# A two-layer encoder trunk: first stage ordered by hand, with operands in PSUM, and per-block statistics in the second layer

## The chip, the cores and the metric

The kernel runs on one NeuronCore of one Trainium2 chip. The metric is the device time of one execution in microseconds, the median of several runs. Engines are named TensorE (PE in the rows), VectorE (DVE), ScalarE (ACT), GpSimd (POOL) and SyncE (SP, which issues the DMAs).

## The reference

512 tokens of width 1024 go through two layers. A conditioning vector c gives per layer six vectors of shifts, scales and gates, `silu(c) @ w_mod + b_mod`. In each layer:

```
h = rms_norm(x, g) * (1 + scale1) + shift1
[q_d | k_d | v_d | c_q | c_kv | k_rope] = h @ w_in
o_d = 8 heads of dilated windowed attention, ALiBi by position, q and k normed per head
o_m = 8 heads of latent attention: normed c_q and c_kv projected up, a rotary key shared by the heads
x = x + gate1 * (concat[o_d, o_m] @ w_out)
h = rms_norm(x, g') * (1 + scale2) + shift2
x = x + gate2 * (relu(h @ w1) ** 2 @ w2)
```

All is float32. The positions are integers; the angles of the rotary part are position times inverse frequency.

## The kernel before

x is kept transposed, eight tiles x0 to x7 of 128 channels by 512 tokens. Every product that needs float32 accuracy is made of three: each operand is split into a high part (a copy to a short format, on ScalarE, L233) and the rest (a subtraction on GpSimd, L234), and `mm3` (L237 to L240) multiplies high by high, low by high and high by low.

The conditioning takes 96 blocks of 512 KB of `w_mod`. silu(c) is spread over all partitions as a row `cb` of 1024 elements: the diagonal of each piece is multiplied by ones on TensorE into PSUM, and ScalarE copies the bank to SBUF (L112 to L118). One VectorE instruction multiplies a block by `cb` and sums it (L170).

The **first stage** (L694 to L753) norms x and projects it. It first sums the squares of x (ScalarE squares, VectorE adds, L122 to L128) while GpSimd works out the rotary angles (L135 to L147) and ScalarE their sine and cosine (L150, L151), for which it loads another set of tables and then loads the set for Ln and Exp again (L152). The inverse norm (`inv_rms`, L244 to L251) is 512 columns wide and ends in an SBUF tile y. Then a loop goes over the eight chunks of 128 channels. Per chunk: two blocks of `w_mod` are multiplied on VectorE (a scale and a shift), u = x times y on VectorE (L719), the high part of h on ScalarE (L732), all of h on ScalarE (L733), the low part on VectorE for one chunk and on GpSimd for the next (L723, L735), and 24 products on TensorE: four blocks of tokens of the first dilated head pair (384 columns, four banks `mm`) and four of the latent projection (416 columns, two banks `sc` and two banks `tr`). For every second chunk the weights are loaded and split.

After the loop come the statistics of the first dilated pair (`chain` in `dil_prep`, L428 to L451: squares, a reduction over two blocks, the small inverse root `rsqrt_tiny` of L221 to L226 with Ln and Exp, a scaling), its transposes (`tail`), the same for the latent part with the rotary key and its tables (`tail` in `latent`, L521 to L542), and the distances of positions (L305 to L325). Then eight steps, one per head pair, run the attention (`heads`, `head`); in each the projection of a later pair, weight loads and blocks of `w_mod` are placed by `weave` at positions from a table. `head` makes scores into a bank `sc` (L472, L473), adds a bias (L339, L343), takes the softmax, transposes it into a bank `tr` (L358), splits it (L361, L362) and multiplies it with the values (L368).

A scheduler orders each engine's instructions by a simulated timeline, within the data's dependences and the buffers' numbers; only VectorE's order in the chunk loop, and some single instructions, are fixed by hand to the order in the program. Tiles with a tag share as many buffers as BUFS gives the tag; a new one waits until an old one is read for the last time.

Of the kernel before, what the change touches and what calls it, by code (L numbers as in the profile page):

```python
# [16 lines left out]
L = 2  # L17
# [25 lines left out]
def trunk(ctx: ExitStack, tc: tile.TileContext, a):  # L43
# [28 lines left out]

    def ps(tag, shape=(128, 512)):
        return psum.tile(list(shape), F32, tag=tag, bufs=BUFS[tag], name=nm(tag))
# [20 lines left out]
    SY.dma_start(inv, bass.AP(tensor=a["inv"].tensor, offset=a["inv"].offset, ap=[[0, 128], [1, 16]]))  # L95
# [8 lines left out]


# [5 lines left out]
    cb = const.tile([128, D], F32, name="cb")  # L111
    for i in range(2):  # L112
        p = ps("sc", (128, 4, 128))
        dg = s2([128, 4, 128])
        for k in range(4):
            V.tensor_scalar(dg[:, k], ident, cs[:, 4 * i + k:4 * i + k + 1], None, op0=OP.mult)
        T.matmul(p.rearrange("p k c -> p (k c)"), ones, dg.rearrange("p k c -> p (k c)"), start=True, stop=True)
        A.activation(cb[:, 512 * i:512 * i + 512], p.rearrange("p k c -> p (k c)"), AF.Copy)  # L118


    sq0 = s2(tag="o")
    for j in range(8):  # L122
        if j == 0:
            A.activation(sq0, xT[j], AF.Square)
        else:
            sq = s2(tag="P")
            A.activation(sq, xT[j], AF.Square)
            V.tensor_tensor(sq0, sq0, sq, op=OP.add)  # L128


    pf = col(4, "pf")
    V.tensor_copy(pf, posc)
    ang, kf, w_ = s2([128, 4, 16]), s2([128, 4, 16]), s2([128, 4, 16], tag="b")
    for t in range(4):
        G.tensor_scalar(ang[:, t], inv, pf[:, t:t + 1], 0.0, op0=OP.mult, op1=OP.add)  # L135
    G.tensor_scalar(kf, ang, 1.0 / (2 * math.pi), 12582912.0, op0=OP.mult, op1=OP.add)
    G.tensor_scalar(kf, kf, -12582912.0, 0.0, op0=OP.add, op1=OP.add)
    c1 = 6.28125
    c2 = float(np.float32(np.round((2 * math.pi - c1) * 2.0 ** 20) / 2.0 ** 20))
    c3 = 2 * math.pi - c1 - c2  # L140
    for cc in (c1, c2, c3):
        G.tensor_scalar(w_, kf, -cc, 0.0, op0=OP.mult, op1=OP.add)
        G.tensor_tensor(ang, ang, w_, op=OP.add)
    PI_ = 3.1415925
    G.tensor_scalar(ang, ang, PI_, -PI_, op0=OP.min, op1=OP.max)
    A.activation(kf, ang, AF.Abs)
    G.tensor_scalar(kf, kf, -1.0, math.pi / 2, op0=OP.mult, op1=OP.add)  # L147
    sin = const.tile([128, 4, 16], F32, name="sin")
    cos = const.tile([128, 4, 16], F32, name="cos")
    A.activation(sin, ang, AF.Sin)  # L150
    A.activation(cos, kf, AF.Sin)  # L151
    pre = A.preload_act_table_set("natural_log_exp_and_others")  # L152
    tc.keep_in_program_order(pre)
    ctx.enter_context(tc.issue_after(pre.ins))
# [7 lines left out]
    def mod_block(l, i, tag="raw", pool_=False, pin=False, out=None):  # L162
        out = modc[l][:, i:i + 1] if out is None else out
        w = t4(tag, [128, D], F32)
        SY.dma_start(w, a["wmod"][l, i])
        if pool_:
# [25 lines left out]
    def first_norm(j):  # L192

        A.activation(modc[0][:, j:j + 1], mraw[:, j:j + 1], AF.Identity, bias=cols[0][:, C_BMOD + j:C_BMOD + j + 1])
        A.activation(amix[0][:, j:j + 1], mraw[:, 8 + j:9 + j], AF.Identity, bias=gb0[:, j:j + 1],
                     scale=cols[0][:, C_GMIX + j:C_GMIX + j + 1])

# [31 lines left out]
    def load_split(src, n, raw="raw"):  # L229
        raw = t4(raw, [128, 1024], F32)[:, :n]  # L230
        hi, lo = t4("wh", [128, 1024])[:, :n], t4("wl", [128, 1024])[:, :n]
        SY.dma_start(raw, src)
        A.activation(hi, raw, AF.Copy)  # L233
        G.tensor_tensor(lo, raw, f(hi), op=OP.subtract)  # L234
        return hi, lo
# [8 lines left out]
    def inv_rms(p, v, y, t):  # L244

        V.tensor_scalar(v, p, 1.0 / D, EPS, op0=OP.mult, op1=OP.add)
        A.activation(t, v, AF.Ln)
# [3 lines left out]
        V.scalar_tensor_tensor(y, t, 1.5, p, op0=OP.add, op1=OP.mult)  # L251
# [52 lines left out]
    def distances():  # L304

        posr = s2([128, S], I32)
        SY.dma_start(posr, bass.AP(tensor=a["pos"].tensor, offset=a["pos"].offset, ap=[[0, 128], [1, S]]))
# [10 lines left out]
        dist = [t4("ot", [128, 2, S], F32) for _ in range(2)]  # L318
        for qb in range(4):
# [3 lines left out]
        g = t4("ot", [128, 896], F32)  # L323
        SY.dma_start(g, a["lnc"])
        return dist, g  # L325
# [52 lines left out]
    for l in range(L):  # L378
# [19 lines left out]
        def group(src, n):  # L398
            ws = {}

            def load(i, raw="raw"):
                hi, lo = load_split(src[i], 2 * n, raw)
                ws[i] = (hi.rearrange("p (k n) -> p k n", k=2), lo.rearrange("p (k n) -> p k n", k=2))

# [4 lines left out]
            return [lambda i=i, **kw: load(i, **kw) for i in range(4)], step  # L409
# [13 lines left out]
        def dil_prep(pr, k_outer=False):  # L423
            w = dict(mm=[], chain=[])
            w["load"], step = group(a["win"][l, pr], 384)
            R = {}

            def chain(tb, bank):  # L428
# [4 lines left out]
                if t == 0:  # L433
                    R[half] = t4("pt" if k_outer else "zz", [128, 2, 4, 2, 64], F32)
                    R["sq"], R["bank"] = s2([128, 8, 64]), bank
                sq = R["sq"]
                A.activation(sq[:, 4 * t:4 * t + 4].rearrange("p h d -> p (h d)"), bank[:, 0:256], AF.Square, scale=1.0 / 8)
                src = bank[:, 256:384].rearrange("p (h d) -> p h d", h=2)
                vt = R["VD"][:, tb]
                A.activation(vt[:, :, 0], src, AF.Copy)  # L440
                V.tensor_tensor(vt[:, :, 1], src, f(vt[:, :, 0]), op=OP.subtract)
                if t == 0:
                    return

                v = small(8)
                V.tensor_reduce(v, sq, axis=AX.X, op=OP.add)
                rs = rsqrt_tiny(v, 8, bank)
                for u, bk in enumerate((R["bank"], bank)):
                    src = bk[:, 0:256].rearrange("p (h o d) -> p h o d", h=4, o=1).to_broadcast([128, 4, 2, 64])
                    scl = rs[:, 4 * u:4 * u + 4].rearrange("p (h o d) -> p h o d", o=1, d=1).to_broadcast([128, 4, 2, 64])  # L450
                    V.tensor_tensor(R[half][:, u], src, scl, op=OP.mult)  # L451
# [48 lines left out]
        def latent():  # L500
            w = dict(mm=[], chain=[])
            w["load"], step = group(a["winc"][l], W_C)
# [191 lines left out]
        if l == 0:  # L694
# [9 lines left out]
            def u_of(k):  # L704
                return us[k // 2][:, k % 2]
# [240 lines left out]
```

## Time and profile before

| what | us |
|---|---|
| median of 3 runs | 1368.05 |
| lowest and highest | 1367.66, 1368.26 |
| the profiled execution | 1368.62 |
| its span in the trace | 1366.8 |
| TensorE busy | 1275.1 (93%) |
| VectorE busy | 752.4 (55%) |
| ScalarE busy | 673.9 (49%) |
| GpSimd busy | 651.0 (48%) |

Times in the trace count from the start of the span. Busy time of TensorE is of pipelined products: one product's duration overlaps the next one's, so their pace is read from the distances of their starts. The first stage lies from 0 to about 80 us, the attention of the first layer to about 340, its second half to about 730, and the second layer behind it.

### The profile page before, as it was taken

What the parts mean: (1) busy time and instruction counts of PE and PEld (TensorE: products, weight loads), DVE (VectorE), ACT (ScalarE), POOL (GpSimd) and SP (SyncE); (2) the same over time, 40 slices, a digit from 0 to 9 for tenths busy, and PEclk for the clock granted to TensorE, in tenths of its full rate; (3) what the DMA queues carried; (4) which work ended last, traced back from release to release, by engine and by line L of the source; (5) the groups of instructions that cost most, each with busy time, mean ns of one, the idle gap of its engine ahead of it and who ended that gap; (6) DMA issues with size and microseconds to landing.
All of it is one profiled execution on the core that took longest, in us unless ns stands there. A gap on an engine that the chain in (4) does not pass through costs nothing.

```text
span 1366.8 us, 19167 instructions
## 1 busy us (share of the span) xinstructions
PE 1275.1 (93%) x6922; PEld 1109.2 (81%) x6922; DVE 752.4 (55%) x1588; ACT 673.9 (49%) x1389; POOL 651.0 (48%) x504
## 2 busy tenths in 40 slices
PE   3879979898899999999998999999889999999999
PEld 2878867787888888888898988788688888888888
DVE  6677888876661752825574566987662122121223
ACT  5567888875532332322344766887654133232321
POOL 5636785571554444444443533454145444444441
PEclk7989999999999999999999999999999999999999
DMA  9325552331163663845522433211013223223321
GB/s 344 111 95 170 181 164 90 118 124 63 63 224 115 218 229 103 294 142 188 170 82 63 132 124 111 74 45 62 1 63 108 93 93 108 93 93 100 101 93 62
DMA packets 57247, 167.59 MB, mean 123 GB/s; under 512 B 8641, under 2 KB 10817, under 8 KB 57153
## 3 DMA queue, kind: packets, MB, share of 16 engines
q1 hardware_dynamic: 57152, 166.38, 37.0%
q8 instruction: 54, 0.88, 0.3%
q14 instruction: 41, 0.33, 0.1%
HBM read 155.87 MB, written 10.49 MB: 122 GB/s over the span
## 4 chain that ended last, share of the span: by engine, by line
PE 72%; DVE 6%; ACT 5%; issue 4%; POOL 4%; DMA 3%; POOLq 0%; DVEq 0%; ACTq 0%
PE mm L238 21%; PE mm L239 21%; PE mm L240 21%; PE tr L368 3%; PE tr L358 2%; POOL wl L234 2%; DMA raw<-in_wout_dram 1%; DVE pt L362 1%; ACT wh L233 1%; DVE P L343 1%; POOL raw L167 1%; PE sc L238 1%; PE mm L459 1%; PE sc L239 1%; PE sc L240 1%
## 5 line engine op out<-in xcount | busy, mean ns | idle before, releaser
L234 POOL TENSOR_TENSOR wl<-raw,wh 128x1024 fp32r<-128x1024 f32 (+3 forms) x188 | 425.4, 2266 | 449.6 <-ACT wh L233 431.4
L233 ACT ACTIVATE wh<-raw 128x1024 fp32r<-128x1024 f32 (+3 forms) x188 | 189.0, 1005 | 273.7 <-PE mm L240 206.4
L649 DVE SCALAR_TENSOR_TENSOR x<-mm,mod,x 128x512 f32<-128x512 f32 (+1 forms) x144 | 89.1, 629 | 259.9 <-PE mm L240 259.5
L238 PE MATMUL mm<-h,wh 128*128 128x512 f32 (+1 forms) x608 | 224.5, 370 | 7.1 <-ACT h L274 7.1
L239 PE MATMUL mm<-h,wl 128*128 128x512 f32 (+1 forms) x608 | 224.6, 370 | 0.0
L240 PE MATMUL mm<-h,wh 128*128 128x512 f32 (+1 forms) x608 | 221.7, 369 | 1.1 <-POOL h L271 1.1
L238 PE MATMUL mm<-ot,wh 128*128 128x512 f32 (+1 forms) x448 | 154.1, 347 | 4.9 <-ACT ot L641 4.1
L239 PE MATMUL mm<-ot,wl 128*128 128x512 f32 (+1 forms) x448 | 153.1, 344 | 0.0
L240 PE MATMUL mm<-ot,wh 128*128 128x512 f32 (+1 forms) x448 | 150.7, 346 | 0.6 <-POOL ot L642 0.6
L822 ACT ACTIVATE P<-mm 128x512 f32<-128x512 f32 (+1 forms) x72 | 39.2, 551 | 203.9 <-PE mm L240 203.9
L238 PEld LDWEIGHTS mm<-h,wh 128*128 128x128 f32 x608 | 116.2, 191 | 26.1 <-ACT h L274 7.5
L239 PEld LDWEIGHTS mm<-h,wl 128*128 128x128 f32 x608 | 116.1, 191 | 19.0 <-POOL wl L234 0.3
L240 PEld LDWEIGHTS mm<-h,wh 128*128 128x128 f32 x608 | 114.5, 190 | 20.3 <-POOL h L271 1.6
L823 DVE SCALAR_TENSOR_TENSOR mm<-mm,P 128x512 f32<-128x512 f32 (+1 forms) x72 | 45.4, 636 | 138.6 <-ACT P L822 138.6
L238 PE MATMUL mm<-wh,h 128*128 128x384 f32 (+1 forms) x288 | 98.7, 357 | 15.8 <-ACT h L732 9.8
L239 PE MATMUL mm<-wh,h 128*128 128x384 f32 (+1 forms) x288 | 101.8, 354 | 5.1 <-POOL h L735 3.6
L238 PE MATMUL mm<-qk,wh 128*128 128x512 f32 (+1 forms) x288 | 105.3, 366 | 1.0 <-DVE x L649 1.0
L239 PE MATMUL mm<-qk,wl 128*128 128x512 f32 (+1 forms) x288 | 105.2, 365 | 0.0
L240 PE MATMUL mm<-qk,wh 128*128 128x512 f32 (+1 forms) x288 | 105.2, 365 | 0.0
L355 POOL TENSOR_SCALAR P<-P,hs 128x512 f32<-128x512 f32 x64 | 48.4, 756 | 116.5 <-DVE hs L348 94.8
L240 PE MATMUL mm<-wl,h 128*128 128x384 f32 (+1 forms) x288 | 100.2, 351 | 0.0
L170 DVE SCALAR_TENSOR_TENSOR pt<-pt,cb 128x1024 f32<-128x1024 f32 x56 | 99.1, 1804 | 0.0
(248 smaller groups left out, 2667.1 us busy)
## 6 DMA issues: line engine op xcount, KB each, us to landing
raw<-in_w_dram SPq DMA_DIRECT2D x64, 512.0 KB, 3.3
pt<-in_wmod_dram SPq DMA_DIRECT2D x56, 512.0 KB, 4.8
raw<-in_w2a_dram SPq DMA_DIRECT2D x48, 512.0 KB, 3.4
raw<-in_wmod_dram SPq DMA_DIRECT2D x24, 512.0 KB, 3.6
raw<-in_win_dram SPq DMA_DIRECT2D x30, 384.0 KB, 3.2
bias<-b SPq DMA_DIRECT2D x32, 256.0 KB, 2.1
raw<-in_wout_dram SPq DMA_DIRECT2D x16, 512.0 KB, 3.4
raw<-in_w2b_dram SPq DMA_DIRECT2D x16, 512.0 KB, 3.3
```

The lines of the kernel that those rows point to most:

```text
L170: r = V.scalar_tensor_tensor(w, w, 1.0, cb, op0=OP.mult, op1=OP.mult, accum_out=out)
L233: A.activation(hi, raw, AF.Copy)
L234: G.tensor_tensor(lo, raw, f(hi), op=OP.subtract)
L238: T.matmul(out, sh, mh, start=first, stop=False)
L239: T.matmul(out, sl, mh, start=False, stop=False)
L240: T.matmul(out, sh, ml, start=False, stop=last)
L355: G.tensor_scalar(P, P, r_, 0.0, op0=OP.mult, op1=OP.add)
L358: T.transpose(tr[:, kc], P[:, kc * 128:(kc + 1) * 128], ident)
L368: T.matmul(po[:, HALF[qh]], vals(hd, kc), pt[qh][w][:, kc], start=(kc == 0 and w == 0), stop=(kc == 3 and w == 1))
L649: V.scalar_tensor_tensor(xT[j][:, hf], p, gt[:, j:j + 1], xT[j][:, hf], op0=OP.mult, op1=OP.add)
L822: A.activation(r, p, AF.Relu)
L823: V.scalar_tensor_tensor(p, p, 0.0, r, op0=OP.max, op1=OP.mult)
```

## The change

In the first stage the order of SP, VectorE, ScalarE and GpSimd is now the program's, written out by hand. The row cb stays in PSUM through the chunk loop (`cbp`, in a tile `trp` of two banks that replaces the two `tr` buffers; later uses of tag `tr` take its halves by turns), and ScalarE copies it to SBUF only behind the loop. The inverse norm stays in PSUM too; its Ln reads the bank itself, with scale and bias. The sum of squares is kept in PSUM until its last addition, and two of the squares are made by GpSimd. The low part of h is made by GpSimd for every chunk. The blocks of `w_mod` come in eight buffers in place of sixteen; the splits of the latent weights use other buffers for the first half.

In the loop, TensorE makes the four blocks of the dilated pair and one block of the latent projection; its other three blocks follow behind the loop, one in the bank that the norm leaves and two in banks `mm`. The angles, the sine (one operation for sine and cosine, with both loads of tables) and the distances stand behind the loop, on VectorE and ScalarE. The tables of the rotary key and the key itself (`rope`) move into the second attention step of layer 1. In layer 2 the dilated statistics are worked out for each block of 128 tokens, where they were for two together.

The diff, cut to its core:

```diff
+    trp = psum.tile([128, 2, 512], F32, name="trp")
+    turn = [0]
     def ps(tag, shape=(128, 512)):
+        if tag == "tr":
+            turn[0] ^= 1
+            v = trp[:, turn[0]]
+            return v.rearrange("p (a b) -> p a b", a=shape[1]) if len(shape) == 3 else v
...
-    cols = [col(N_COL, f"cols{l}") for l in range(L)]
-    SY.dma_start(cols[0], a["cols"][0])
-    posc = const.tile([128, 4], I32, name="posc")
-    SY.dma_start(posc, a["pos"].rearrange("(t p) -> p t", p=128))
-    inv = col(16, "inv")
-    SY.dma_start(inv, bass.AP(tensor=a["inv"].tensor, ...))
     xT = [const.tile([128, S], F32, name=f"x{j}") for j in range(8)]
     for j in range(8):
         SY.dma_start(xT[j], a["xT"][j])
+    cols = [col(N_COL, f"cols{l}") for l in range(L)]
+    SY.dma_start(cols[0], a["cols"][0])
...
+    cbp = trp.rearrange("p a b -> p (a b)")
     for i in range(2):
...
-        A.activation(cb[:, 512 * i:512 * i + 512], p.rearrange("p k c -> p (k c)"), AF.Copy)
+        T.matmul(cbp[:, 512 * i:512 * i + 512], ones, dg.rearrange("p k c -> p (k c)"), start=True, stop=True)
...
+    def rotary():
+        pf = col(4, "pf")
+        V.tensor_copy(pf, posc)
+        ang, kf = sin, cos
+        for t in range(4):
+            V.tensor_scalar(ang[:, t], inv, pf[:, t:t + 1], None, op0=OP.mult)
+        V.tensor_scalar(kf, ang, 1.0 / (2 * math.pi), 12582912.0, op0=OP.mult, op1=OP.add)
+        V.tensor_scalar(kf, kf, -12582912.0, None, op0=OP.add)
...
+        for cc in (c1, c2, c3):
+            V.scalar_tensor_tensor(ang, kf, -cc, ang, op0=OP.mult, op1=OP.add)
...
+        A.activation(sines, sines, AF.Sin)
+        exp_tables()
...
-    def inv_rms(p, v, y, t):
+    def inv_rms(p, v, t):
+        A.activation(t, p, AF.Ln, bias=epsc, scale=1.0 / D)
         V.tensor_scalar(v, p, 1.0 / D, EPS, op0=OP.mult, op1=OP.add)
-        A.activation(t, v, AF.Ln)
         A.activation(p, t, AF.Exp, scale=-0.5)
...
-        V.scalar_tensor_tensor(y, t, 1.5, p, op0=OP.add, op1=OP.mult)
+        V.scalar_tensor_tensor(p, t, 1.5, p, op0=OP.add, op1=OP.mult)
...
-    def distances():
-        posr = s2([128, S], I32)
+    def distances(posr):
...
+        rotary()
         for qb in range(4):
...
+                nb = 2 if l == 0 else 1
+                if t == 0 or nb == 1:
+                    R["sq"], R["bank"] = s2([128, 4 * nb, 64]), []
...
+                if len(got) == nb:
+                    v = small(4 * nb)
+                    V.tensor_reduce(v, sq, axis=AX.X, op=OP.add)
+                    rs = rsqrt_tiny(v, 4 * nb, bank)
+                    for u, (t_, bk) in enumerate(got):
...
+                        V.tensor_tensor(R[half][:, t_], src, scl, op=OP.mult)
...
+            with tc.manual_schedule(engines={E.SP, E.DVE, E.Activation, E.Pool}):
+                for k in range(8):
+                    mods(k)
+                    if k % 2 == 0:
+                        weights(k // 2)
+                    if k == 2:
+                        SY.dma_start(posc, a["pos"].rearrange("(t p) -> p t", p=128))
...
+                sq0, sqp = s2(tag="o"), ps("mm")
+                A.activation(sqp, xT[0], AF.Square)
+                for j in range(1, 8):
+                    sq = s2(tag="P")
+                    if j in (1, 4):
+                        G.tensor_tensor(sq, xT[j], xT[j], op=OP.mult)
+                    else:
+                        A.activation(sq, xT[j], AF.Square)
+                    V.tensor_tensor(sq0 if j == 7 else sqp, sqp, sq, op=OP.add)
+                T.matmul(p, ones, sq0, start=True, stop=True)
+                banks = [ps("mm") for _ in range(4)]
+                lbanks = [ps("sc")]
+                splits(0)
+                mod_mul(8)
+                mod_mul(0)
+                inv_rms(p, v, t)
+                for k in range(8):
...
+                    V.tensor_tensor(u, xT[k], p, op=OP.mult)
+                    first_norm(k)
+                    A.activation(hi, u, AF.Identity, bias=be, scale=ga)
+                    A.activation(u, u, AF.Identity, bias=be, scale=ga)
+                    G.tensor_tensor(lo, u, f(hi), op=OP.subtract)
+                    if k % 2 == 0 and k < 6:
+                        splits(k // 2 + 1)
                     if k < 7:
...
+                        mod_mul(9 + k)
+                        mod_mul(k + 1)
+                    for tb in range(4):
+                        PR[0]["step"](banks[tb][:, :384], k, tb)
+                    W["step"](lbanks[0][:, :W_C], k, 0)
+                gains()
+                dist = distances(posr)
+                for i in range(2):
+                    A.activation(cb[:, 512 * i:512 * i + 512], cbp[:, 512 * i:512 * i + 512], AF.Copy)
+            lbanks.append(ps("sc"))
+            for k in range(8):
+                W["step"](lbanks[1][:, :W_C], k, 1)
+            g = t4("ot", [128, 896], F32)
+            SY.dma_start(g, a["lnc"])
+            bias0 = dist, g
+            for fn in PR[1]["load"][:2]:
+                fn(keep=True)
             for tb in range(4):
                 PR[0]["do_chain"](tb, banks[tb])
+            for tb in (2, 3):
+                lbanks.append(ps("mm"))
+                for k in range(8):
+                    W["step"](lbanks[tb][:, :W_C], k, tb)
...
+            if l == 0 and st == 1:
+                ev += [(2, W["rope"])]
```

## Rows read from the trace of the kernel before

**Rows 1.** stages; busy PE, PEld, DVE, ACT, POOL; clock, DMA share, GB/s

```profile
25.50:70.30 44.80, 39.94 (x192) 37.30 (x192) 33.75 (x46) 24.93 (x47) 28.87 (x23) 0.92 0.46 165
70.30:79.40 9.10, 4.13 (x19) 3.40 (x20) 7.79 (x22) 6.69 (x29) 3.30 (x2) 0.81 0.46 151
79.40:100.00 20.60, 18.55 (x88) 17.61 (x87) 15.36 (x44) 12.47 (x37) 8.00 (x9) 0.83 0.21 74
100.00:180.00 80.00, 74.88 (x464) 69.52 (x462) 64.70 (x153) 63.86 (x146) 56.55 (x41) 0.98 0.52 171
180.00:220.00 40.00, 30.31 (x197) 24.52 (x194) 30.57 (x86) 35.73 (x86) 34.19 (x35) 0.91 0.50 156
```

**Rows 2.** TensorE in order of time: start us, us, engine, line, operation

```profile
25.55 0.69 PE L238 MATMUL mm<-wh,h 128*128 128x384 f32 x1 [9.48 <-ACT h L732]
...
69.76 0.35 PE L239 MATMUL tr<-wh,h 128*128 128x416 f32 x1
69.94 0.35 PE L240 MATMUL tr<-wl,h 128*128 128x416 f32 x1
...
79.43 0.47 PE L472 MATMUL sc<-qk,qk 128*128 128x512 f32 x1
```

**Rows 3.** ScalarE in order of time, front of the program and last chunk

```profile
15.60 1.28 ACT L150 ACT_TABLE_LOAD   x1
...
19.82 0.61 ACT L247 ACTIVATE b<-b 128x512 f32<-128x512 f32 x1
...
24.68 0.81 ACT L732 ACTIVATE h<-pt,mod,am 128x512 fp32r<-128x512 f32 x1 [2.98 <-DVE pt L728]
...
59.62 0.81 ACT L732 ACTIVATE h<-pt,mod,am 128x512 fp32r<-128x512 f32 x1
```

**Rows 4.** VectorE's groups, 24 to 60 us: count, busy us, mean ns

```profile
L170 DVE SCALAR_TENSOR_TENSOR qk<-qk,cb 128x1024 f32<-128x1024 f32 x7 | 11.5, 1646 | 0.0
L170 DVE SCALAR_TENSOR_TENSOR ot<-ot,cb 128x1024 f32<-128x1024 f32 x7 | 9.6, 1374 | 0.0
L719 DVE TENSOR_TENSOR pt<-x,P 128x512 f32<-128x512 f32 x7 | 9.1, 1304 | 0.0
L723 DVE TENSOR_TENSOR h<-pt,h 128x512 fp32r<-128x512 f32 x4 | 4.1, 1037 | 1.4 <-ACT pt L733 1.4
```

**Rows 5.** VectorE in order of time, chunk loop

```profile
24.56 0.68 DVE L719 TENSOR_TENSOR pt<-x,P 128x512 f32<-128x512 f32 x1
...
45.03 0.68 DVE L719 TENSOR_TENSOR pt<-x,P 128x512 f32<-128x512 f32 x1
45.64 1.21 DVE L170 SCALAR_TENSOR_TENSOR qk<-qk,cb 128x1024 f32<-128x1024 f32 x1
```

**Rows 6.** GpSimd in order of time, end of the chunk loop

```profile
58.14 2.82 POOL L234 TENSOR_TENSOR wl<-zz,wh 128x768 fp32r<-128x768 f32 x1
...
63.98 1.85 POOL L234 TENSOR_TENSOR wl<-raw,wh 128x768 fp32r<-128x768 f32 x1
...
65.79 1.28 POOL L735 TENSOR_TENSOR h<-pt,h 128x512 fp32r<-128x512 f32 x1
```

**Rows 7.** VectorE's largest group from 100 to 300 us

```profile
L362 DVE TENSOR_TENSOR pt<-tr,pt 128x512 fp32r<-128x512 f32 x51 | 34.4, 683 | 8.1 <-ACT pt L361 7.9
```

**Rows 8.** DMA rate from 0 to 42 us, 40 slices of 1.05 us

```profile
GB/s 0 1 84 19 79 239 392 396 392 388 417 410 421 407 410 416 406 406 410 401 400 414 417 406 414 390 412 401 413 417 402 414 410 410 399 376 391 407 249 19
```

**Rows 9.** SP's queue in order of time, front of the program

```profile
1.84 0.42 SPq L91 DMA_DIRECT2D cols<-in_cols_dram  x1
...
3.33 0.43 SPq L99 DMA_DIRECT2D x<-in_xT_dram  x1
```

**Rows 10.** VectorE's groups from 60 to 94 us

```profile
L322 DVE SCALAR_TENSOR_TENSOR ot<-pt,pc,ot 128x512 f32<-128x512 f32 x4 | 3.8, 1005 | 0.0
```

**Rows 11.** VectorE's groups from 735 to 890 us, second layer

```profile
L446 DVE TENSOR_REDUCE st<-s 128x8 f32<-128x512 f32 x7 | 4.8, 685 | 1.9 <-ACT s L437 1.9
```

**Rows 12.** TensorE's waits, 800 to 980 us: total, times, longest

```profile
PE sc L472 <- DVE hs L343: 8.3, 7, 1.8
```

More of the change, by code (lines that the diff above doesn't have):

```diff
@@ L227, in rsqrt_tiny, with split, load, load_split @@
         return r
-    def load_split(src, n, raw="raw"):
-        raw = t4(raw, [128, 1024], F32)[:, :n]
[L231 to L235, printed above, removed]
+    def split(raw, n, tags=("wh", "wl"), keep=False):
+        hi, lo = t4(tags[0], [128, 1024])[:, :n], t4(tags[1], [128, 1024])[:, :n]
+        ra = A.activation(hi, raw, AF.Copy)
+        rg = G.tensor_tensor(lo, raw, f(hi), op=OP.subtract)
+        if keep:
+            tc.keep_in_program_order(ra)
+            tc.keep_in_program_order(rg)
+        return hi, lo
+    def load(src, n, raw="raw", keep=False):
+        raw = t4(raw, [128, 1024], F32)[:, :n]
+        r = SY.dma_start(raw, src)
+        if keep:
+            tc.keep_in_program_order(r)
+        return raw
+    def load_split(src, n, keep=False):
+        return split(load(src, n, keep=keep), n, keep=keep)
     def mm3(out, sh, sl, mh, ml, first, last):
@@ L399, in group, with put, load @@
             ws = {}
-            def load(i, raw="raw"):
-                hi, lo = load_split(src[i], 2 * n, raw)
+            def put(i, hi, lo):
                 ws[i] = (hi.rearrange("p (k n) -> p k n", k=2), lo.rearrange("p (k n) -> p k n", k=2))
+            def load(i, keep=False):
+                put(i, *load_split(src[i], 2 * n, keep))
             def step(bank, k, tb):
@@ L407, in step @@
                     ws[k // 2][0][:, k % 2], ws[k // 2][1][:, k % 2], k == 0, k == 7)
-            return [lambda i=i, **kw: load(i, **kw) for i in range(4)], step
+            return [lambda i=i, **kw: load(i, **kw) for i in range(4)], step, put
         def blocks(w, n, step, chain):
@@ L442, in chain @@
[L442 to L451, printed above, removed]
+                nb = 2 if l == 0 else 1
@@ new lines, in chain, with values @@
+                if t == 0 or nb == 1:
+                    R["sq"], R["bank"] = s2([128, 4 * nb, 64]), []
+                sq, got = R["sq"], R["bank"]
+                got.append((t, bank))
+                A.activation(sq[:, 4 * len(got) - 4:4 * len(got)].rearrange("p h d -> p (h d)"), bank[:, 0:256],
+                             AF.Square, scale=1.0 / 8)
+                def values():
+                    src = bank[:, 256:384].rearrange("p (h d) -> p h d", h=2)
+                    vt = R["VD"][:, tb]
+                    A.activation(vt[:, :, 0], src, AF.Copy)
+                    V.tensor_tensor(vt[:, :, 1], src, f(vt[:, :, 0]), op=OP.subtract)
@@ L453, in tail @@
+                if nb == 1:
+                    values()
             def tail(half):
@@ L741, in trunk, with mods, weights, splits @@
-            gains()
+            ml, wr = {}, {}
+            def mods(k):
+                ml[8 + k] = mod_load(0, 8 + k, "qk")
+                ml[k] = mod_load(0, k, "qk")
+            def weights(i):
+                raw = ("raw", "zz")[i % 2]
+                wr[i] = load(a["win"][0, 0, i], 768, raw), load(a["winc"][0, i], 2 * W_C, raw)
+            def splits(i):
+                PR[0]["put"](i, *split(wr[i][0], 768))
+                W["put"](i, *split(wr[i][1], 2 * W_C, ("ot", "ot") if i < 2 else ("wh", "wl")))
@@ L745, in trunk @@
+            for fn in PR[0]["tail"]:
                 fn()
@@ L747, in trunk @@
                 W["do_chain"](tb, lbanks[tb])
-            for fn in PR[0]["tail"]:
-                fn()
             W["tail"]()
-            bias0 = distances()
             for l2 in range(1, L):
```

136 lines of the change are left out of this document (43 added, 93 removed).

## The prediction

> **What bounds the kernel now.** The profiled execution took 1368.62 us (span 1366.8), 0.57 above the median 1368.05; the sum below is made on its span and moved to the median at the end. I read first the busy time by stage, then for the first stage each engine in order of time, then the waits of TensorE. The stages show TensorE full nearly everywhere but at the front: from 25.5 to 70.3 us it is busy 39.9 of 44.8 us, in the 9.1 us after that 4.1, and until 100 us its granted clock is 0.81 to 0.92 [rows 1]. [...] It starts late (first product 25.55), ends late (last 69.94), and the first score follows 9.5 us behind, at 79.43 [rows 2].
>
> Two things make it late. The first h needs the inverse norm, whose Ln stands at 19.82 on ScalarE behind the tables for the sine (a load is 1.28 us, the first at 15.60) [rows 3]. Then VectorE paces the chunks, and not at its own speed: the multiplications by cb, u and lo of chunks 1 to 7 take 11.5 + 9.6 + 9.1 + 4.1 = 34.3 us [rows 4], while singly they take 1.21 and 0.68 [rows 5]; 14 x 1.21 + 7 x 0.68 + 4 x 0.68 = 24.4 us. The missing 10 us lie where GpSimd runs its subtractions beside them, and those grow too: one of 768 columns took 2.82 us there, another, undisturbed, 1.85 [rows 6]. An operation of VectorE that reads PSUM shows none of it: 51 in the attention stage, where GpSimd is busy most of the time, mean 0.683 us [rows 7]. DMA is at 390 to 420 GB/s until about 40 us [rows 8], so chunks can't come much faster than VectorE at its own speed would take them.
>
> **The change, part by part.**
> *Queue.* Three small loads go behind x: x is issued from 3.33, the first of the three at 1.84 [rows 9], so the stream starts 1.5 us earlier and the last chunk's two blocks land near 38.5 instead of 40. SP is written out by hand now: blocks 12 and 4 wait for a buffer that multiplications 8 and 0 free before the first u, so I take no stall there.
> *Start.* Sine, its tables and the angles leave the front; two squares go to GpSimd; the Ln reads the bank itself. Two split copies still stand ahead of it, and wait for their weights. The first h (24.68 [rows 3]) comes at 19.5 by my estimate, 5.2 us earlier. Bounds: 1.5 (the queue alone) and 6.5 (the queue and all that Ln lost since 15.60, less one load's 1.28, and no more than the DMA lets through).
> *Chunk loop.* With cb and the inverse norm in PSUM, and lo wholly on GpSimd, VectorE has 0.68 + 2 x 1.21 = 3.1 us a chunk, 22 us for seven. u of chunk 7 is then at 18.7 + 21.8 = 40.5 to 41.2; by the DMA 38.5 + 2 x 1.21 + 0.68 = 41.6. I take h of chunk 7 at 42; it was at 59.62 [rows 3]. The PSUM form of the 1024-wide multiplication is not in the trace; by the 512-wide row it costs what the SBUF form costs. [...] GpSimd now has eight lo at 1.28 and four pairs of splits at 1.85 to 2 [rows 6], about 25 us beside VectorE's 22: nearly full, but the first pair of splits comes ahead of the loop, and subtractions that VectorE no longer disturbs keep to 1.28 and 1.85.
> *End of the loop.* Before, lo of chunk 7 ended at 67.07, 7.5 us behind its h, since splits stood ahead of it on GpSimd [rows 6]; now 0.81 + 0.81 + 1.28, at 45. Only 15 products a chunk remain in the loop, so TensorE ends it at 47.5 instead of 69.94.
> *What is moved behind it.* 72 products of the latent projection, 13.3 us at full clock: block 1 at once (to 52), blocks 2 and 3 when the first pair's banks come free. The chain of that pair is where the added wait sits: its Ln must follow the sine and the reload of the tables (two loads, 2.6 us) on ScalarE, and the sine follows the angles on VectorE, behind u of chunk 7. Queued behind are the four distances (3.8 us before, with GpSimd beside [rows 10]) and the copies of cb, and the first transposes need those copies, which release both banks. All of it lies beside products of block 1; cost between 0 (covered) and 8 us (in series), taken at 2, as the cover is 4.4 us long. So banks at 53, blocks 2 and 3 to 62, first score at 63 against 79.43: **16.4 us**. The 9.5 us of waiting behind the loop are filled with products that were in it: that is the main gain. If the cover failed, blocks 2 and 3 would start late and TensorE would stand idle as now.
> *Give-back.* The tables for the rotary key go into stage 1, to GpSimd, some 14 small operations, and the latent statistics now run beside the first scores, where two of the projection's weights also keep buffers that the second dilated projection waits for. Between 0 and 6, taken at 2. The small loads that move with all this (positions, the mask's table, two gains) are one issue of about 0.4 us each on SP [rows 9], which then stands waiting for buffers: nothing, as long as the weights behind them have their buffers late anyway. Stage 180 to 220 (ScalarE 35.7 of 40, TensorE 30.3) [rows 1] shows where a shift can be lost.
> *Second layer.* Statistics per block: eight pairs each get a second Ln, Exp and three small operations, and two half reductions in place of one of 0.685 [rows 11]; a bank comes free one block earlier. TensorE waits there 8.3 us for score banks in 800 to 980, for VectorE [rows 12]. More small work there costs up to 4 us, an earlier bank gains up to 2; taken at 0.
> *Turns of the transpose banks.* A fixed pair instead of two buffers: the same two banks in the same order, nothing, unless the halves are not kept apart (below).
> Sum: 16.4 - 2 = 14.4 us; 1368.62 - 14.4 - 0.57 = 1353.7, said as **1353.5**.
>
> **Rivals.**
> *The rest takes it up* (1362). The attention stage of layer 1 ends a wait on ScalarE or GpSimd rather than on TensorE; what is won in front is waited for in 180 to 220 [rows 1]. For: ScalarE is 89% busy there. Against: from 100 to 180 TensorE is the full engine, and a filler product is mostly ready. Gain 6 us.
> [...]
> *Slower* (1390). The two halves of the new two-bank PSUM tile are tracked as one. Then transposes of a block wait until ScalarE and VectorE have read the block before, and the double buffer is gone in both layers: 128 groups and 32 products with the values, each up to the 0.68 us of VectorE's reading [rows 7]. At a third of it, the rest covered by projections, 160 x 0.23 = 37 us. It decides from 14.4 / 160 = 0.09 us each. Against: u of chunk 1 was written at 24.56 into the tile whose other half ScalarE read from 24.68 [rows 3, 5], so halves of an SBUF tile are apart; no PSUM tile of before spans two banks.
> *It doesn't do what it says* (1366.7). The banks for blocks 2 and 3 are taken late, the sine holds the chain in series (8 instead of 2) and GpSimd paces the loop (lo of chunk 7 six us late): the first score at 76, and 3.4 us less the 2 of give-back.
>
> **How the numbers follow.** Forecast 0.53, smaller gain 0.19, larger gain 0.19, slower 0.05, no effect 0.04. The range 1343 to 1363 holds the forecast with the bounds of start, cover, give-back and second layer (1348 to 1360), most of the smaller gain and rather over half of the larger: 8 in 10. A measurement of this kernel can tell about 0.2%, 2.7 us, from no change: faster by over that 0.91 (the first three, and none of the others), within it 0.04, slower 0.05.
>
> **What would show it.** Right: operations of VectorE in the loop at 1.2 to 1.3 and 0.68 us whatever GpSimd does; GpSimd's splits at 1.85; first product near 20, end of the loop near 47, first score near 63; TensorE idle below 4 us between 48 and 63. [...]

## The result, and the profile after

The changed kernel takes 1529.24 us (median of 4 runs, 1528.20 to 1532.66) against 1367.94 for the kernel before: ratio 1.1176, 95% interval 1.1151 to 1.1201. It is 161 us slower where 14 us less was forecast. The page of the changed kernel, busy time of TensorE and its granted clock in 40 slices:

```profile
PE 1336.0 (88%) x6922; PEld 1144.7 (75%) x6922; DVE 750.8 (49%) x1628; ACT 686.3 (45%) x1401; POOL 635.1 (42%) x496
...
PEclk9899989967799999999999998898669999999999
```

TensorE has the same number of products, spread over a longer span, and its clock falls in two places, slices 9 to 11 and 25 to 30 of the 40 (of 38 us each): the attention of the first and of the second layer. VectorE's last step of each head (the sum of the two halves of its output) dates the stages. All 32 of them before, with the start of the first and of the last:

```profile
L371 DVE TENSOR_TENSOR o<-tr,o x32: 672/684/685, 116.1 to 984.3; 64x512 f32<-64x512 f32 x32
```

The same of the changed kernel:

```profile
L382 DVE TENSOR_TENSOR o<-trp,o x32: 673/683/685, 112.4 to 1143.3; 64x512 f32<-64x512 f32 x32
```

The last of layer 1 starts at 328.93 before and at 409.66 now, 80.7 us later; layer 2 adds another 78.3. These are 159.0 of the 159.6 us by which the span grew. It is dearest where few projections stand between the blocks: the last head of layer 1 took 6.7 us before, from the sum of the head ahead of it to its own,

```profile
322.22 0.68 DVE L371 TENSOR_TENSOR o<-tr,o 64x512 f32<-64x512 f32 x1 [0.94 <-ACT o L370]
328.93 0.68 DVE L371 TENSOR_TENSOR o<-tr,o 64x512 f32<-64x512 f32 x1 [1.82 <-ACT o L370]
```

and takes 15.0 now:

```profile
394.70 0.68 DVE L382 TENSOR_TENSOR o<-trp,o 64x512 f32<-64x512 f32 x1 [2.16 <-ACT o L381]
409.66 0.68 DVE L382 TENSOR_TENSOR o<-trp,o 64x512 f32<-64x512 f32 x1 [4.50 <-ACT o L381]
```

The stages of the changed kernel, as in [rows 1], and two more:

```profile
25.50:70.30 44.80, 33.47 (x154) 31.50 (x154) 35.55 (x89) 31.34 (x71) 28.49 (x27) 0.89 0.55 205
...
100.00:180.00 80.00, 67.65 (x391) 60.72 (x390) 48.74 (x116) 51.07 (x113) 43.37 (x34) 0.96 0.42 133
180.00:220.00 40.00, 27.11 (x145) 22.16 (x144) 28.07 (x75) 28.15 (x66) 28.56 (x33) 0.83 0.48 155
220.00:340.00 120.00, 92.83 (x506) 75.99 (x506) 73.33 (x183) 76.29 (x178) 58.92 (x75) 0.88 0.28 92
340.00:440.00 100.00, 69.77 (x409) 60.20 (x410) 43.86 (x97) 42.16 (x87) 23.37 (x23) 0.82 0.15 48
```

From 220 us on no engine is full: TensorE has 92.83 of 120 us, ScalarE 76.29, VectorE 73.33. That is a chain of single steps, not a bound engine. TensorE's waits over the whole span name its links (total, times, longest):

```profile
PE sc L252 <- ACT P L358: 51.2, 39, 2.2
PE trp L369 <- DVE o L382: 29.0, 19, 2.9
PE sc L495 <- DVE hs L354: 23.0, 24, 2.3
```

Transposes into one half wait for VectorE's reading of the other. It is plainest in the last head of layer 1, where no other work lies between: each block's transposes wait 1.4 to 1.5 us for the reading (L373) of the block before, and 2.6 us lie between their starts,

```profile
397.51 1.12 PE L369 MATMUL trp<-ident,P 128*128 128x128 f32 x4 [1.41 <-DVE pt L373]
400.13 1.08 PE L369 MATMUL trp<-ident,P 128*128 128x128 f32 x4 [1.50 <-DVE pt L373]
```

while in the kernel before the same head runs the transposes of two blocks (x8) without a wait between them:

```profile
322.96 1.35 PE L358 MATMUL tr<-ident,P 128*128 128x128 f32 x8 [1.03 <-DVE o L371]
```

How a block runs in the unbiased heads, by ScalarE, VectorE and TensorE in order of time:

```profile
352.48 0.72 ACT L362 ACTIVATE P<-P,hs 128x512 f32<-128x512 f32 x1 [0.23 <-DVE hs L359]
353.75 0.60 ACT L372 ACTIVATE pt<-trp 128x512 fp32r<-128x512 f32 x1 [0.55 <-PE trp L369]
...
351.61 0.69 DVE L373 TENSOR_TENSOR pt<-trp,pt 128x512 fp32r<-128x512 f32 x1 [0.25 <-ACT pt L372]
352.28 0.16 DVE L359 RECIPROCAL hs<-hs 128x1 f32<-128x1 f32 x1
...
354.38 0.69 DVE L373 TENSOR_TENSOR pt<-trp,pt 128x512 fp32r<-128x512 f32 x1 [1.35 <-ACT pt L372]
...
352.30 0.50 PE L252 MATMUL sc<-h,h 96*128 96x512 f32 x1 [1.35 <-ACT P L358]
...
353.11 0.60 PE L369 MATMUL trp<-ident,P 128*128 128x128 f32 x4
...
355.07 0.50 PE L252 MATMUL sc<-h,h 96*128 96x512 f32 x1 [1.36 <-ACT P L358]
```

Reading of the bank (L373) 0.69, reciprocal 0.16, normalisation (L362) 0.72, transposes 0.60, ScalarE's copy (L372) 0.60: together 2.77 us, and 2.77 is the distance of two L373 and of two first score products. Here the wait doesn't stand at the transposes themselves: reciprocal and normalisation of the next block are queued behind the reading of the block before, and TensorE's idle time stands ahead of the next scores. Each block runs behind the reading of the block before; the double buffer is gone.

The first stage, ScalarE and then TensorE in order of time, answering to [rows 2, 3]:

```profile
21.35 0.81 ACT L777 ACTIVATE h<-pt,mod,am 128x512 fp32r<-128x512 f32 x1 [2.50 <-DVE pt L775]
...
47.08 0.82 ACT L777 ACTIVATE h<-pt,mod,am 128x512 fp32r<-128x512 f32 x1
...
48.76 1.28 ACT L152 ACT_TABLE_LOAD   x1
53.51 0.31 ACT L152 ACTIVATE sines<-sines 128x128 f32<-128x128 f32 x1 [3.46 <-DVE sines L151]
...
62.75 0.36 ACT L225 ACTIVATE st<-st,eps 128x8 f32<-128x8 f32 x1
...
57.56 0.34 PE L254 MATMUL sc<-wl,h 128*128 128x416 f32 x1
65.25 0.69 PE L252 MATMUL mm<-ot,h 128*128 128x416 f32 x1 [7.35 <-DVE pt L472]
...
80.98 0.48 PE L495 MATMUL sc<-qk,qk 128*128 128x512 f32 x1
```

The first h comes 3.3 us earlier and h of chunk 7 12.5 us earlier, the last product of the loop and of block 1 is at 57.56, and yet the first score stands at 80.98, 1.5 us later than before. VectorE's groups from 20 to 50 us answer to [rows 4]:

```profile
L741 DVE SCALAR_TENSOR_TENSOR qk<-qk,trp 128x1024 f32<-128x1024 f32 x14 | 16.8, 1217 | 2.7 <-DMA qk<-in_wmod_dram 2.5
L775 DVE TENSOR_TENSOR pt<-x,sc 128x512 f32<-128x512 f32 x8 | 5.5, 683 | 0.0
```

### The profile page after: what moved, and what is told of

It reads as the page before. It is cut to its first block, busy times and chain, and to the rows that moved or that the text cites. A ratio compares the mean times of both kernels' runs of the same rounds, so it can differ in the third digit from the quotient of the medians.

```text
span 1526.4 us, 19278 instructions
## 1 busy us (share of the span) xinstructions
PE 1336.0 (88%) x6922; PEld 1144.7 (75%) x6922; DVE 750.8 (49%) x1628; ACT 686.3 (45%) x1401; POOL 635.1 (42%) x496
## 4 chain that ended last, share of the span: by engine, by line
PE 73%; ACT 8%; DVE 8%; DMA 5%; issue 3%; POOL 3%; SPq 0%; DVEq 0%; ACTq 0%; POOLq 0%
PE mm L252 20%; PE mm L254 20%; PE mm L253 20%; PE trp L379 4%; PE trp L369 3%; PE sc L252 2%; ACT P L358 2%; ACT pt L372 1%; POOL wl L235 1%; ACT wh L234 1%; DVE P L354 1%; DVE pt L373 1%; DMA raw<-in_winc_dram 1%; PE sc L253 1%; DMA raw<-in_wout_dram 1%
## 5 line engine op out<-in xcount | busy, mean ns | idle before, releaser
L235 POOL TENSOR_TENSOR wl<-raw,wh 128x1024 fp32r<-128x1024 f32 (+3 forms) x187 | 421.1, 2256 | 481.7 <-ACT wh L234 464.4
L252 PE MATMUL mm<-ot,wh 128*128 128x512 f32 (+1 forms) x448 | 158.4, 355 | 6.1 <-ACT ot L666 4.1
L254 PE MATMUL mm<-ot,wh 128*128 128x512 f32 (+1 forms) x448 | 151.7, 349 | 0.0
L373 DVE TENSOR_TENSOR pt<-trp,pt 128x512 fp32r<-128x512 f32 x128 | 88.1, 688 | 95.9 <-ACT pt L372 95.4
L369 PE MATMUL trp<-ident,P 128*128 128x128 f32 x512 | 91.1, 307 | 38.8 <-DVE o L382 29.0
L372 ACT ACTIVATE pt<-trp 128x512 fp32r<-128x512 f32 x128 | 76.4, 597 | 95.0 <-PE trp L369 93.1
L369 PEld LDWEIGHTS trp<-ident,P 128*128 128x128 f32 x512 | 69.2, 158 | 61.9 <-issue 28.7
L252 PE MATMUL mm<-wh,h 128*128 128x384 f32 (+1 forms) x296 | 100.5, 354 | 13.9 <-ACT h L777 8.6
L366 POOL TENSOR_SCALAR P<-P,hs 128x512 f32<-128x512 f32 x64 | 44.3, 692 | 162.0 <-DVE hs L359 150.6
L253 PE MATMUL mm<-wh,h 128*128 128x384 f32 (+1 forms) x296 | 104.6, 354 | 3.4 <-POOL h L779 2.3
L252 PE MATMUL mm<-qk,wh 128*128 128x512 f32 (+1 forms) x288 | 105.3, 366 | 1.0 <-DVE x L674 1.0
```

What stands on the lines that cost most here:

```text
L235: rg = G.tensor_tensor(lo, raw, f(hi), op=OP.subtract)
L252: T.matmul(out, sh, mh, start=first, stop=False)
L253: T.matmul(out, sl, mh, start=False, stop=False)
L254: T.matmul(out, sh, ml, start=False, stop=last)
L366: G.tensor_scalar(P, P, r_, 0.0, op0=OP.mult, op1=OP.add)
L369: T.transpose(tr[:, kc], P[:, kc * 128:(kc + 1) * 128], ident)
```

## The experiments

**Is it the two-bank tile?** The theory: its halves are tracked as one. The rivals: another part of the change costs the time, or the fixed turns do.

```
 (kernel before)
+    trp = psum.tile([128, 2, 512], F32, name="trp")
+    turn = [0]
     def ps(tag, shape=(128, 512)):
+        if tag == "tr":
+            turn[0] ^= 1
+            v = trp[:, turn[0]]
+            return ...
```

> The kernel before with one edit: the two buffers of the transposes become the two halves of one two-bank PSUM tile, used in turns (nothing of the new first stage, nothing of the second layer's statistics). Theory (the halves are tracked as one tile, so each block's transposes wait for the last reading of the block before): 1500 to 1545, attention of layer 1 and of layer 2 each some 80 us longer, a wait of the transposes for VectorE's last reading in most blocks. Rival A (the loss comes from the new first stage or the second layer's statistics): 1366 to 1372. Rival B (fixed turns cost, not the single tile): also 1500 or more, told apart by the next run.

1548.46 us, ratio 1.1271 (1.1223 to 1.1319), a little above the range of the theory. These few lines alone cost more than the whole change, 0.1271 x 1369.6 = 174 us (168 to 181 by the interval). Its waits of TensorE are those of the changed kernel:

```profile
PE sc L245 <- ACT P L354: 50.1, 40, 1.4
...
PE trp L365 <- DVE o L378: 25.6, 17, 2.9
```

Next, the same turns on two tiles of one bank each:

```
+    two = [psum.tile([128, 512], F32, name=f"trp{i}") for i in range(2)]
...
+            v = two[turn[0]]
```

> The kernel before with the transposes on two separate one-bank tiles in the same fixed turns as in the run before. Theory (one tile): 1365 to 1372, as before. Rival B (the fixed turns are what costs): 1500 or more.

1367.89 us, ratio 0.9990 (0.9977 to 1.0003). The wait that was 25.6 us is 5.5, as good as the 5.2 of the kernel before:

```profile
PE trp L365 <- DVE o L378: 5.5, 8, 1.2
```

Same turns, same two banks' worth of memory; only that they are one tile costs 174 us. What in the tracking joins the halves was not tried, nor how much of the 174 us is waiting on the chip and how much the scheduler's order, which follows the same dependences.

Third, the changed kernel, repaired (called the repaired kernel from here on): the two-bank tile lives in a pool of its own, which ends when silu's row has been copied; two ordinary buffers follow in its place.

```
-    trp = psum.tile([128, 2, 512], F32, name="trp")
+    first = tc.tile_pool(name="first", bufs=1, space=bass.MemoryType.PSUM)
+    trp = first.__enter__().tile([128, 2, 512], F32, name="trp")
...
+            first.__exit__(None, None, None)
+            tpool["tr"] = ctx.enter_context(tc.tile_pool(name="late", bufs=1, space=bass.MemoryType.PSUM))
```

> The changed kernel, whole, but its two-bank tile lives only until silu's row is copied to SBUF; then two ordinary one-bank buffers take its place for the transposes. Theory: the 160 us vanish, and what is left is the true worth of the rest. The first score of the changed kernel stood at 80.98, later than before (79.43), so I expect little of the forecast 14 us: 1352 to 1369. Rival A: 1515 to 1530, as the changed kernel.

1357.76 us, ratio 0.9905 (0.9890 to 0.9920). And the same with the second layer's statistics per pair again:

```
-                nb = 2 if l == 0 else 1
+                nb = 2
```

> As the run before, with the second layer's dilated statistics per pair of blocks again, as in the kernel before. Forecast step (second layer taken at 0, bounds 4 slower to 2 faster for statistics per block): within 2 us of the run before it; if per-block statistics cost, this one is up to 4 us faster. Rival A gives no difference either, at 1515 to 1530.

1370.23 us, ratio 0.9994 (0.9984 to 1.0003), 12.5 us slower than the repaired kernel. This missed both expectations. All that the repaired kernel gains comes from the step that I had put at nothing, and the first stage gives nothing.

**The second layer.** Per-block statistics alone, in the kernel before:

```
+                nb = 2 if l == 0 else 1
...
-                if t == 0:
-                    return
...
+                if len(got) == nb:
```

> The kernel before with one edit: the second layer's dilated statistics per block, as in the changed kernel. Theory (all that the repaired kernel gains comes from here, and the first stage is worth about nothing): 1355.5 to 1359, TensorE's wait of score products for VectorE in 800 to 980 below 1 us instead of 8.6. Rival (the gain needs the new first stage too): 1364 to 1370.

1358.12 us, ratio 0.9910 (0.9895 to 0.9926): the whole gain, by the smallest edit. The attention of the second layer in the kernel before, from its first score to the end of the last head's sum (busy times and clock as in [rows 1]):

```profile
746.67:985.00 238.33, 223.52 (x1408) 201.59 (x1408) 173.64 (x449) 171.93 (x418) 94.51 (x115) 0.98 0.26 79
```

The same with statistics per block:

```profile
745.27:972.82 227.55, 218.26 (x1408) 197.66 (x1408) 173.89 (x472) 173.20 (x431) 94.94 (x115) 1.00 0.27 82
```

What is left there of the wait of [rows 12], 800 to 980 us:

```profile
PE sc L482 <- DVE hs L343: 0.6, 2, 0.4
```

The wait falls from 8.3 us to 0.6 (the 8.6 of the expectation is that of the whole stage). TensorE's idle time in the stage falls by less, from 14.8 us to 9.3, since its transposes now wait longer for VectorE (4.8 us against 2.4 from 800 to 980); the other half of the 10.8 us by which the stage is shorter goes with the granted clock, 0.98 before and 1.00 now, about 5 us by my estimate (0.02 x 238). VectorE has no less work (173.89 us and 173.64 before). But in the kernel before a pair's reduction, three small operations and two scalings come in one lump, and a bias reduction (L343), which releases a score bank, stands behind parts of it:

```profile
845.04 0.69 DVE L446 TENSOR_REDUCE st<-s 128x8 f32<-128x512 f32 x1 [0.40 <-ACT s L437]
...
846.51 0.67 DVE L343 CUSTOM_DVE_ANT_0 P<-sc,b 128x512 f32<-128x512 f32 x1
...
847.24 0.50 PE L472 MATMUL sc<-qk,qk 128*128 128x512 f32 x1 [1.81 <-DVE hs L343]
```

An earlier free bank of the projection is not what helps: in the kernel before, TensorE waited for none from 800 to 980 us; its 11.1 us of waits there are all ahead of scores, transposes and products with the values. That the spreading does it, and not the new place of the values, the next run shows: per block, but values ahead of the statistics as before (the edit is against the run just shown).

```
-                if nb == 2:
-                    values()
+                values()
...
-                if nb == 1:
-                    values()
```

> The kernel before with the second layer's dilated statistics per block, but each block's values split off ahead of its statistics, as in the kernel before (the changed kernel does it behind them). Theory (the spreading of VectorE's work over the blocks gives the gain): 1356 to 1360. Rival (the new order of the values gives it): 1366 to 1371.

1359.53 us, ratio 0.9920 (0.9903 to 0.9937), as the theory has it. In the first layer score products hardly wait for VectorE from 100 to 180 us (0.3 us in the repaired kernel, 4.7 from 80 to 220); there, in the repaired kernel:

```
-                nb = 2 if l == 0 else 1
+                nb = 1
```

> The repaired kernel (own pool for the two-bank tile) with the statistics per block in the first layer as well. In that layer score products hardly wait for VectorE (0.3 us in 100 to 180 of the repaired kernel), so by the theory that per-block statistics take away just this wait it changes little: 1355 to 1361. Rival (an earlier free bank is what helps, in either layer): 1347 to 1353.

1357.54 us, ratio 0.9905 (0.9884 to 0.9927), no difference from the repaired kernel.

**Why the first stage gives nothing.** In the repaired kernel TensorE still stands 7.27 us behind the loop and the first score is at 78.07. First the sine was put inside the loop and the distances behind the first pair's statistics:

```
-        rotary()
...
                         mod_mul(k + 1)
+                    if k == 3:
+                        rotary()
...
-                dist = distances(posr)
...
                 PR[0]["do_chain"](tb, banks[tb])
+            dist = distances(posr)
```

> The repaired kernel with angles, sine and both table loads inside the chunk loop (behind chunk 3), and the distances behind the statistics of the first pair. TensorE's idle 7.3 us behind the loop (54.6 to 61.8 in the repaired kernel) shrinks to below 3, and the first score comes at 70 to 74 instead of 78.07. Theory (what is won in front is taken up by the attention of the first layer, whose fourth head ends at 168 with either first stage): 1355 to 1359. Rival (the front counts once its idle time is gone): 1347 to 1352.

1363.79 us, ratio 0.9947 (0.9934 to 0.9959), a miss. ScalarE's queue in the loop shows why:

```profile
34.77 1.28 ACT L151 ACT_TABLE_LOAD   x1
40.47 0.31 ACT L151 ACTIVATE sines<-sines 128x128 f32<-128x128 f32 x1 [4.42 <-DVE sines L150]
...
42.70 0.81 ACT L775 ACTIVATE h<-pt,mod,am 128x512 fp32r<-128x512 f32 x1
```

The sine waits for angles that VectorE makes between its multiplications, and the next h stands behind it. The first score was at 79.55. Then the first pair's statistics were put ahead of distances and sine, all by hand:

```
+                for tb in range(4):
+                    PR[0]["do_chain"](tb, banks[tb])
                 dist = distances(posr)
...
-            for tb in range(4):
-                PR[0]["do_chain"](tb, banks[tb])
```

> The repaired kernel with the first pair's statistics ahead of the distances, the angles and the sine, by the order written out by hand (the chunk loop is as in the repaired kernel, so the stall of 4.9 us that the sine made inside the loop can't return). TensorE's idle 7.3 us behind the loop goes to below 2; the first score comes at 66 to 73 instead of 78.07. If the forecast of the front was right but for its cover, the time falls with the first score: 1348 to 1353. If the attention of the first layer takes it up: 1355 to 1359.

1363.18 us, ratio 0.9950 (0.9938 to 0.9962), slower than either forecast, with the first score at 78.69 and not at 66 to 73. TensorE in order of time in this kernel:

```profile
56.98 0.42 PE L251 MATMUL mm<-ot,h 128*128 128x416 f32 x1 [0.54 <-DVE pt L471]
...
71.62 1.97 PE L481 MATMUL mm<-ident,pt 128*128 128x128 f32 x8 [4.45 <-DVE qk L490]
...
78.28 0.66 PE L549 MATMUL mm<-ident,zz 128*128 128x128 f32 x2 [4.69 <-DVE zz L536]
```

The 7.27 us are gone (0.54), and come back as 4.45 and 4.69 further on, since the sine, the distances and the evacuations of the transposes still stand in a row on ScalarE and VectorE. Third, the sine at the very front, as early as the kernel before begins its angles, with the positions loaded ahead of x, and the distances behind the statistics as above:

```
...
+    rotary()
     modc = ...
...
-        rotary()
         for qb in range(4):
...
```

> The repaired kernel with the angles and the sine at the very front, ahead of the squares (as the kernel before has them near the front), and the distances behind the first pair's statistics: nothing but the copies of silu's row then stands between the chunk loop and those statistics, and no sine stands between them and the second pair's banks. First h about 3 us later than in the changed kernel (24 against 21.35), TensorE's idle behind the loop below 2 instead of 7.3, first score at 70 to 75 instead of 78.07. If the forecast of the front failed only because that idle time stayed: 1349 to 1354. If the first layer's attention takes up whatever is won in front: 1355 to 1359, with the fourth head again at 167 to 170.

1357.44 us, ratio 0.9900 (0.9878 to 0.9923). Here the first score does come earlier:

```profile
60.30 0.43 PE L255 MATMUL mm<-ot,h 128*128 128x416 f32 x1 [1.35 <-DVE pt L474]
...
74.14 0.73 PE L497 MATMUL sc<-qk,qk 128*128 128x512 f32 x2 [0.92 <-ACT qk L488]
```

And the time is the same within the noise, as the second theory said: 0.7 us less than the repaired kernel, give or take 3.7 by the two intervals, for a first score that is 3.9 us earlier. Its six runs lie from 1351.33 to 1359.71, and the traced one is the slowest. One table of all, one traced execution each: first score; end of the last head's sum in layer 1; from there to the end of that of layer 2 (by VectorE's rows, us).

| kernel | first score | layer 1 ends | to layer 2's end |
|---|---|---|---|
| before | 79.43 | 329.61 | 655.4 |
| repaired, statistics per pair | 78.50 | 328.81 | 656.9 |
| before, second layer per block | 78.11 | 328.61 | 644.2 |
| repaired | 78.07 | 328.09 | 645.8 |
| sine in the loop | 79.55 | 335.69 | 644.5 |
| sine behind the statistics | 78.69 | 335.01 | 645.5 |
| sine in front | 74.14 | 330.72 | 645.8 |

The last column separates cleanly, 644 to 646 with statistics per block and 655 to 657 without. The middle one doesn't follow the first: first scores from 78.07 to 79.55 go with ends between 328 and 336, and the earliest first score with an end at 331.

**What takes it up?** Two theories, both on queues between 98 and 118 us. First GpSimd: normalisations stand there behind splits and biases. They were moved to VectorE in the biased heads of layer 1, in the kernel with the sine in front and in a control.

```
-NRM = (('AAGG', 'GAGA'), ('GAGA', 'GAVG'))
+NRM = (('AAGG', 'VAVA'), ('GAGA', 'GAVG'))
```

> The kernel with the sine in front (first score 74.1), with one edit: in the first layer's biased heads the normalisations of blocks 0 and 2 go from GpSimd to VectorE (0.69 us each on GpSimd; there they stand in its queue behind weight splits of 1.8 to 2.8 us and biases of 1.3, and the transposes waited 4.2 us for one at 112). Theory (GpSimd takes up what is won in front): the time falls by 2 to 6 us against its parent's 1357.4, to 1351.5 to 1355.5, and the fourth head ends before 168. Rival (VectorE or TensorE's own work takes it up): within 2 us of its parent, or slower.

> The control: the kernel before with the second layer's statistics per block (1358.1), and the same two normalisations moved to VectorE. Theory: there transposes wait less for GpSimd (1.2 us at the longest), so it moves by less than 2 us. Rival: it moves by as much as the run before it, so the edit's worth has nothing to do with the front.

1359.17 us, ratio 0.9922 (0.9901 to 0.9943), no better than its parent's 0.9900; the control 1365.28 us, 0.9958 (0.9943 to 0.9973), some 7 us slower than its own 0.9910 where less than 2 was forecast. The forecast of a gain failed; as the edit has a cost of its own in the control, the pair doesn't rule GpSimd out. Then ScalarE: split copies of the next pair's weights wait there for their transfer. They were put one block later, and fixed there in the program's order, in three kernels:

```
-                ev += spread(PR[st + 2]["load"], tn("LD0"), tn("LD1"))
+                if l == 0:
...
+                    for p0, i in spread(range(4), tn("LD0"), tn("LD1")):
+                        ev += [(p0, ...load...), (p0 + 1, ...split...)]
...
```

> The repaired kernel (own pool) with one edit in the first layer: the weights of pairs 2 and 3 are loaded where they were, but their split copies stand one block of a head later in ScalarE's and GpSimd's program. In the repaired kernel ScalarE waited 4.0 us in 98 to 118 for those weights with exponentials, normalisations and evacuations queued behind, and TensorE was busy 0.99 of 5 us in 105 to 110. Theory (this queue takes up what the front wins): ScalarE's wait for the weights there goes below 1 us, TensorE busy above 3.5 of 5 us in 105 to 110, fourth head at 162 to 166 instead of 168.1, time 1350 to 1355. Rival (something else takes it up): 1356 to 1360, fourth head at 167 to 170.

> The same edit on the kernel with the sine in front (1357.4, first score 74.1). Theory: 1349 to 1354. Rival: 1356 to 1360.

> Control: the same edit on the kernel before with the second layer's statistics per block (1358.1; ScalarE waits 1.8 us for those weights). Theory: within 2 us of 1358, since there is little to take away. Rival: it gains as much as the two runs with the new front.

1364.46 us, 0.9955 (0.9937 to 0.9973); 1366.23 us, 0.9964 (0.9948 to 0.9979); the control 1373.41 us, 1.0018 (1.0004 to 1.0032). All three are slower than either forecast, by 7, 9 and 15 us against their parents. In the first of them ScalarE's wait for the weights was gone and the fourth head ended at 158.3 instead of 168.1, yet TensorE was busy 1.99 of the 5 us from 105 to 110 and not 3.5, and layer 1 ended at 333.1; in the control the fourth head ended at 160.1 too, and layer 1 at 345.8. So the gain forecast from this queue is not there, and a single head's end is no measure; but as this edit also costs in the control, these runs can't say that the queue takes up nothing. What takes the front up stays open. For the traced executions the table shows that it is taken up; the times of all runs show only that little of it arrives.

The fastest versions are four within each other's intervals, at 0.990 to 0.991: the repaired kernel, the same with the first layer per block too, the one with the sine in front, and the kernel before with nothing but the second layer's statistics per block, which is the simplest.

## Why the prediction was wrong

**Turns of the transpose banks**, "the same two banks in the same order, nothing", is the step that failed. It cost 174 us in the run with that step alone. The mechanism stood there as the rival *Slower*, with a chance of 0.05 and 37 us. The chance rested on an SBUF tile whose halves are apart [rows 3, 5]; that does not carry over to this PSUM tile, and the text itself said that no PSUM tile of before spans two banks. The price was far too low: a third of the 0.68 us of VectorE's reading [rows 7] per use, 0.23 us, where 174 / 160 = 1.09 us were measured. What is lost is not a part of one reading: a block's whole way through three engines, 2.77 us, stands behind the block before, and the projections that should have covered it don't follow densely enough: from 220 to 440 us TensorE is busy 162.6 of 220 us, and gets a clock of 0.82 to 0.88.

**Start.** The first h came at 21.35 instead of 19.5: 3.3 us gained, within the bounds. The first of the two split copies ahead of the Ln waited 2.96 us for its weights, until 14.47.

**Chunk loop.** Its prices were right: 1217 and 683 ns in the mean, where GpSimd works beside it for 21.3 of the 30 us from 20 to 50. The multiplication took 1.217 us with `cb` in PSUM, against 1.21 from SBUF [rows 5]. The length was not right: h of chunk 7 at 47.08 and not 42. *Queue* had taken no stall, but ScalarE's longest wait in the loop was one of 3.9 us for a pair's weights, ahead of the next h, VectorE waited 2.5 us for blocks, and SP waited 5.7 us in six waits for earlier blocks before it issued more.

**What is moved behind it** is the second step that failed: 2 us for the sine's chain, "as the cover is 4.4 us long". That cover was not there: block 1 of the latent projection ran in the gaps of the loop and ended with it, at 57.56. The idle time was 7.35 us, near the upper end of 8. The products behind it started 0.35 us apart until 69, at a granted clock of 0.50, and 0.19 apart from there on, at 1.00 from 70 to 72 us. Then transposes, their evacuations and the latent statistics followed, which the forecast had at 1 us (62 to 63) and which took from 76.19 to 80.98. So 63 became 80.98, and the gain of 16.4 us a loss of 1.5. With the sine in front the first score was 5.3 us earlier than before, and the time (0.9900) no better than without any new front (0.9910) within the intervals. That is the rival *The rest takes it up*, if not in its place.

**Second layer**, taken at 0 with bounds from 4 slower to 2 faster, gave 12 us: 8.3 us stood in [rows 12], I let an earlier bank win 2 of them, and the clock that went with the waits was left out. The wait was for VectorE, and the question should have been how its work is spread, not when a bank comes free.

The terms now add up: +174 for the turns (168 to 181), -12 for the second layer, about -1 for the front (0.9905 for the repaired kernel against 0.9910 without its front, less than the intervals can tell from nothing): +161, as measured. That it comes out to the microsecond is luck, with an interval of 13 us on the first term. The repaired kernel's 1357.76 lies in the range of 1343 to 1363, but that would have been luck too: its gain is the second layer's, taken at nothing, and not the first score's 16.4 us.

## What to carry to other kernels

Ask of a new tile that holds two buffers whether its halves are kept apart in this memory; where no row shows it, price the loss of the double buffer as the whole way of one block through all engines, less the pace that the blocks had with it, times the uses, and give it the chance of an unknown. Where an engine's wait is written out in a row (8.3 us for VectorE), the bound of an edit that touches that engine's queue is the whole row and the clock lost with it (about 5 us here). An earlier start of a stage is a gain only if the end of that stage moves, so look at that end first.

## What was not expected of the hardware

The waits of up to 1.8 us for score banks in the second layer went with a granted clock of 0.98 over the stage, and with them nearly gone it was 1.00: of the 10.8 us by which the stage is shorter, about 5 are clock by my estimate, and TensorE's idle time gives only 5.5. And the same products with almost the same first score ended layer 1 anywhere from 328 to 336 us in kernels that differ only in the order of the first stage, so one trace of a reordered front says little about what the front is worth.
